# Order of the last out projections in the first mixing, and the point where the second feed-forward's modulation stream starts

## The chip, the core and the metric

One core of a Trainium2 chip runs the whole program. The metric is device time in microseconds (us). The kernel before took 1815.4 us, the median of three runs (1815.14 to 1818.62). Engines are named as in the profile: PE is TensorE's matmul and PEld its weight load, DVE is VectorE, ACT is ScalarE, POOL is GpSimd, SP is the queue that issues nearly all DMAs.

## What is computed

Two layers of a hybrid backbone. A stream of 256 latent tokens `x` and a stream of 256 context tokens `xc`, each 1024 wide, go through: a modulated SwiGLU feed-forward, a token mixing, a second modulated feed-forward. Only the latents are put out, so the context stops after layer 1's keys and values. What matters here is the end of layer 0's mixing and the feed-forward behind it:

```python
x = x + mx[5] * y                      # y = (attention outputs) @ w_out
x = x + 0.5 * mx[8] * swiglu(modulate(rms_norm(x), mx[6], mx[7]), *ffn2)
if need_ctx:                           # layer 0
    xc = xc + mc[5] * y_c
    xc = xc + 0.5 * mc[8] * swiglu(modulate(rms_norm(xc), mc[6], mc[7]), *ffn2)
```

`mx` and `mc` are nine modulation vectors per layer, made from the conditioning vectors by a 1024 by 9216 matrix `w_mod`.

## The kernel before, in words

Activations lie transposed: `xT[k]` holds features 128k to 128k+127 of all 512 tokens, latents in columns 0 to 255 (half `v` = 0), context in 256 to 511 (`v` = 1). Every matmul is done as three, since each operand is split into a high and a low float32r part (`mm3`; the high part is written by ACT, the low part by DVE, or for a few blocks by POOL). A weight block is loaded by `wcols` into `raw` (three buffers), split into `hs` (five buffers), and used by 24 matmuls for each 128 by 512 stretch.

The mixing of layer 0, `mix0`, is a set of named items that `run` carries out in the order of the string `MIX0`. The items `of<dp><v>` are the last out projections: block `dp` of 256 output features, token half `v`. Each has two groups of six matmuls into `ops`, and for each group `residual` adds the result to `xT` (DVE, line 295), squares it (ACT, lines 301 and 304) and adds the square to `ssum` (DVE, line 96). The last item of a half calls `norm_half`: `norm_stats` sums `ssum` over the features with matmuls into `nst`, takes the inverse root (DVE and ACT operations `xe`, `nt`, `rs`), and `norm_bcast` spreads it with two diagonal tiles `dg` (DVE) and two matmuls into `nbc`. `norm_apply` then writes `hT[k]` for k = 0 to 7 with `nrm` (DVE), the high part (ACT) and the low part (DVE). For `v` = 1 that last step is put in a list and run by `flush` inside the first pair of the feed-forward.

`ffn` computes gate (`gps`) and up (`ups`) products pair by pair. Its first pair is "halved": 96 matmuls of 256 columns for the latents, 96 for the context; later pairs have 96 matmuls of 512 columns each.

The modulation vectors that are not needed at the start are computed on DVE: `mod_part` multiplies a row block of `w_mod` with the conditioning vector and sums (`junk`, line 212), one operation for each of the two conditioning vectors. `pump_every` sets how many of these are written behind each block of matmuls. For the second feed-forward of layer 0 the first of them stands behind a gate: a copy of one element of `xT[7][:, 255:256]` into `junk` (line 209), which can only run once that element has its final value.

The code is traced by Python, and a scheduler then lays each engine's instructions into one fixed order by priority and its own idea of when operands are ready; engines carry them out in that order and wait on semaphores. So the table and the gate decide what the scheduler may put where.

At the end of layer 1's mixing, `raw_chunk` writes the un-normed input `hTl` of the last feed-forward chunk by chunk; columns 256 and 257 of `hTl` hold the shift vector twice. They are written by two ACT copies (line 368) and two DVE subtractions (line 369).

Of the kernel before, what the change touches and what calls it, by code (L numbers as in the profile page):

```python
# [8 lines left out]
F32 = mybir.dt.float32  # L9
R32 = mybir.dt.float32r  # L10
I32 = mybir.dt.int32
AF = mybir.ActivationFunctionType
# [6 lines left out]
KC = 8  # L19
SEQ = 256  # L20
NTOK = 512
# [4 lines left out]
HALF = (slice(0, 256), slice(256, 512))  # L26
FFN_PARTS = (6, 5)
MOD_STEP = 1
GATE = lambda xT: xT[7][:, 255:256]


POOL = """of21 od30 of20 oa01 dk00 dv10 uq1 bk11 uk00 oa20 bq00 oa30 aq11 uk01 ob30 ob10 dq00 bk10 oc20 dv11 ob31 oa00
# [20 lines left out]

MIX0 = """g bq00 bk00 f bk01 bv00 bq01 bq10 sb0b sb0a bk10 sb1b sb1a bq11 bv01 rb0 bk11 rb1 sb2a ak0 sb2b bv10 bv11
    sb3a rb2 ak1 aq00 aq01 sb3b rb3 aq10 sa1 sa0 aq11 ob30 sa2 ob31 ob10 ob11 ra0 sa3 ra2 sa4 sa5 ra1 ra3 ob20
    ra4 oa31 sa6 sa7 ob00 ob21 oa10 ob01 oa30 ra6 oa01 oa21 oa00 ra7 oa11 ra5 oa20 of11 of21 of00 of10 of30 of31
    of01 of20"""
MIX1 = """dq00 cq00 g f dk00 dk01 sd0 sd2 dv00 dv01 cq20 rd0 sd1 sd3 cq10 dk10 cqn dq10 rd2 dk11 sd6 rd1 uq0 dv10 dv11
    sd5 sd4 sd7 ckv0 rd4 rd3 ckv1 uk10 rd5 uk00 rd6 uk11 rd7 uk01 uq1 sc0 rc0 od00 sc1 sc2 sc4 sc3 od10 sc6 rc1
    rc2 sc5 od20 rc3 sc7 rc4 rc6 rc5 oc00 rc7 oc30 oc20 of20 of30 of00 oc10 of10 od30"""  # L60
# [3 lines left out]
def tile_hybrid_dit(ctx: ExitStack, tc: tile.TileContext, I, out, dbg=None):  # L64
    nc = tc.nc
    V, S, T, Q = nc.vector, nc.scalar, nc.tensor, nc.sync
# [72 lines left out]
    def const(name, shape, src=None):  # L139
        n = math.prod(shape[1:])  # L140
        at, size = place.get(SHARED.get(name), (sum(z for _, z in place.values()), n))
        assert n <= size and at + n <= NCONST
        if name not in SHARED:
            place[name] = at, n
        t = call[:, at:at + n]
        if len(shape) > 2:
            ax = "abcd"[:len(shape) - 1]
            t = t.rearrange(f"p ({' '.join(ax)}) -> p {' '.join(ax)}", **dict(zip(ax, shape[1:])))
        if src is not None:
            Q.dma_start(out=t, in_=src)  # L150
        return t
# [13 lines left out]
    modT = const("modT", [P, 2, 2, 9, KC])  # L165
# [25 lines left out]
    def needs_ctx(l, m):  # L191

        return l == 0 or m < 5
# [11 lines left out]
    def mod_part(l, m, k, raw):  # L205

        junk = rawp.tile([P, D], F32, tag="junk", name="junk", bufs=1)
        if mod_gate[0] is not None:
            V.tensor_copy(junk[:, 0:1], mod_gate[0])
            mod_gate[0] = None  # L210
        for v in range(2 if needs_ctx(l, m) else 1):
            V.tensor_tensor_reduce(out=junk, in0=raw, in1=mod_c[v], scale=0.5 if m in (2, 8) else 1.0,  # L212
                                   scalar=bT[:, l, m, k:k + 1], op0=ALU.mult, op1=ALU.add,
                                   accum_out=modT[:, l, v, m, k:k + 1])

    def mod_stream():

        raw = None
        while mod_list:
            l, m = mod_list.pop(0)  # L220
            for k in range(KC):
                if raw is None:
                    raw = mod_load(l, m, k)
                    yield
                now, raw = raw, None
                nxt = (l, m, k + 1) if k + 1 < KC else mod_list[0] + (0,) if mod_list else None
                if nxt is not None:
                    raw = mod_load(*nxt)
                mod_part(l, m, k, now)
                if k + 1 == KC:  # L230
                    mod_done.add((l, m))
                yield

    mod_list, mod_gen, mod_gate = [], [None], [None]

    def need(l, *ms):
        while any((l, m) not in mod_done for m in ms):
            pump(1)

    def queue_mods(l, *ms):  # L240
        if not mod_list:
            mod_c.clear()
        mod_list.extend((l, m) for m in ms)
# [39 lines left out]
    xT = [xall[:, k, :] for k in range(KC)]  # L283
    ssum = const("ssum", [P, NTOK])
    hT = [None] * KC
# [74 lines left out]
    hraw = []  # L360

    def raw_chunk(l, m, k):
        need(l, m, m + 1)
        if not hraw:
            hraw.append(hp.tile([P, KC, 2, 264], R32, tag="hTl", name="hTl", bufs=1))
            sh = modT[:, l, 0, m, :].rearrange("p (k o) -> p k o", o=1)
            for c in (256, 257):
                S.activation(hraw[0][:, :, 0, c:c + 1], sh, AF.Copy)
                V.tensor_tensor(out=hraw[0][:, :, 1, c:c + 1], in0=sh, in1=hraw[0][:, :, 0, c:c + 1].bitcast(F32),
                                op=ALU.subtract)  # L370
        h, x, sc = hraw[0][:, k, :, 0:256], xT[k][:, 0:256], modT[:, l, 0, m + 1, k:k + 1]
        S.activation(h[:, 0], x, AF.Copy, scale=sc)
        V.scalar_tensor_tensor(out=h[:, 1], in0=x, scalar=sc, in1=h[:, 0].bitcast(F32), op0=ALU.mult,  # L373
                               op1=ALU.subtract)

# [612 lines left out]
    def mix1():  # L988
# [261 lines left out]
        for h in range(8):  # L1250
            d_unit(h)
            c_unit(h)
        put("", out_items(1, w_out, {"od": (od, 4, (0, 1, 2, 3), None), "oc": (oc, 0, (0, 1), OUT_TAGS[2]),
                                     "of": (oc, 0, (2, 3), OUT_TAGS[3])}, (0,), lambda v: raw_stats(1, 6), lambda k: raw_chunk(1, 6, k)))
        run(items, MIX1)

# [3 lines left out]
    def probe():  # L1260
        if dbg is not None:
            for k in range(KC):
                Q.dma_start(out=dbg[f"x{k}"], in_=xT[k])
# [13 lines left out]
    next(mixing[0], None)  # L1277
    if stop == 1:
        return probe()
    mod_gate[0] = GATE(xT)  # L1280
    queue_mods(0, 8)
    queue_mods(1, 1, 0, 2)
    ffn(0, *w(0, 2), 8, (0, 1), lambda v: norm_half(1, 0, v))
# [58 lines left out]
```

## Time and profile before

| | |
|---|---|
| median of three runs | 1815.4 us |
| the profiled execution's own time | 1815.71 us |
| its span, first to last instruction | 1813.6 us |
| mean granted TensorE clock | 0.993 of 2.4 GHz |
| PE busy, share of the span | 97% |
| DVE busy, share of the span | 67% |
| ACT busy, share of the span | 41% |

The span is what the trace covers; the 2.1 us between it and the execution's own time lie around it. Times inside the trace are us from the span's start. In a row of the timeline the bracket at the end names how long the engine sat idle before that row and which instruction of which engine ended the wait.

### The profile page before, as it was taken

The page shows a single profiled execution, that of the slowest core. Times are in us where ns is not written, and L with a number is a line of the kernel's source. Part 1 is how long each engine was busy: PE and PEld are TensorE (multiplying, and loading weights), DVE is VectorE, ACT ScalarE, POOL GpSimd, SP SyncE. Part 2 cuts the span into 40 slices and gives each one's busy share as a digit, 9 for nine tenths or more (in the row PEclk, how much of TensorE's full clock was granted, in tenths as well). Part 3 has the DMA queues.
Part 4 walks back from the last instruction along what each step waited for, and adds up shares of the span by engine and source line. Part 5 has one row for each costly group of instructions (what it writes and reads, how often), then busy time and mean ns, then how long its engine had stood idle before and what let it go on. Part 6 is the DMA issues. An engine that isn't in the chain of part 4 may idle for free.

```text
span 1813.6 us, 26777 instructions
## 1 busy us (share of the span) xinstructions
PE 1762.3 (97%) x10563; PEld 1537.5 (85%) x10563; DVE 1220.6 (67%) x2343; ACT 738.8 (41%) x1322; POOL 46.0 (3%) x25
## 2 busy tenths in 40 slices
PE   7999999999999989999999999999999998999999
PEld 5788888898998888888888988888889986789998
DVE  5999953467688699989854633333346787876664
ACT  4333132345666543222233332222334656664442
POOL 0000000011010000000000000000001011000000
PEclk9999999999999989999999999999999999999999
DMA  9777752322110237778863233233233442155552
GB/s 305 273 245 225 236 190 88 116 73 68 50 60 14 59 121 240 241 229 261 300 199 105 81 94 94 92 105 103 88 111 101 89 102 57 47 178 183 175 186 82
DMA packets 214025, 256.90 MB, mean 142 GB/s; under 512 B 21484, under 2 KB 195724, under 8 KB 213900
## 3 DMA queue, kind: packets, MB, share of 16 engines
q1 hardware_dynamic: 213900, 255.19, 45.6%
q8 instruction: 83, 1.36, 0.3%
q14 instruction: 42, 0.34, 0.1%
HBM read 254.11 MB, written 1.05 MB: 141 GB/s over the span
## 4 chain that ended last, share of the span: by engine, by line
PE 87%; DVE 7%; ACT 3%; DMA 2%; issue 1%; SPq 0%; DVEq 0%; ACTq 0%
PE ups L103 23%; PE gps L103 23%; PE dps L103 23%; PE ops L103 3%; PE po L756 2%; PE sc L103 2%; DVE hs L100 1%; DMA bias<-in_d_rpb_dram 1%; PE trp L659 1%; PE pbk L103 1%; PE pbv L103 1%; PE paq L103 1%; PE pbq L103 1%; PE ptl L724 1%; PE mps L524 1%
## 5 line engine op out<-in xcount | busy, mean ns | idle before, releaser
L100 DVE TENSOR_TENSOR hs<-raw,hs 128x1024 fp32r<-128x1024 f32 (+2 forms) x308 | 367.9, 1200 | 284.1 <-ACT hs L99 283.4
L99 ACT ACTIVATE hs<-raw 128x1024 fp32r<-128x1024 f32 (+2 forms) x308 | 314.9, 1030 | 541.4 <-PE dps L103 177.8
L103 PE MATMUL dps<-ah,hs 128*128 128x512 f32 (+1 forms) x2256 | 401.0, 338 | 0.2 <-DVE hs L100 0.2
L103 PEld LDWEIGHTS dps<-ah,hs 128*128 128x128 f32 x2256 | 350.6, 190 | 46.4 <-DVE hs L100 0.4
L103 PE MATMUL gps<-hT,hs 128*128 128x512 f32 (+1 forms) x1680 | 375.3, 380 | 4.9 <-ACT hT L542 2.7
L103 PE MATMUL ups<-hT,hs 128*128 128x512 f32 (+1 forms) x1680 | 371.6, 377 | 0.0
L103 PEld LDWEIGHTS gps<-hT,hs 128*128 128x128 f32 x1680 | 305.0, 190 | 65.5 <-ACT hT L542 3.5
L103 PEld LDWEIGHTS ups<-hT,hs 128*128 128x128 f32 x1680 | 303.3, 188 | 58.8 <-issue 1.0
L212 DVE CUSTOM_DVE_ANT_0 junk<-mraw,cb,const 128x1024 f32<-128x1024 f32 x224 | 283.6, 1283 | 16.3 <-DMA mraw<-in_k_w_modT_dram 11.1
L99 ACT ACTIVATE ah<-af 128x512 fp32r<-128x512 f32 (+1 forms) x88 | 50.4, 574 | 127.5 <-DVE af L93 93.9
L295 DVE SCALAR_TENSOR_TENSOR xT<-dps,const,xT 128x256 f32<-128x256 f32 x112 | 50.3, 480 | 77.0 <-PE dps L103 76.9
L276 POOL TENSOR_TENSOR hs<-raw,hs 128x1024 fp32r<-128x1024 f32 (+2 forms) x21 | 45.8, 2186 | 1558.2 <-ACT hs L275 1493.8
L93 DVE TENSOR_TENSOR af<-sg,ups 128x512 f32<-128x512 f32 x66 | 45.2, 685 | 41.0 <-PE ups L103 40.9
L103 PE MATMUL gps<-hTl,hs 128*128 128x258 f32 x528 | 66.8, 284 | 1.6 <-DVE hTl L373 1.0
L428 ACT ACTIVATE sg<-gps 128x512 f32<-128x512 f32 x66 | 38.9, 589 | 70.2 <-PE gps L103 70.2
L103 PEld LDWEIGHTS gps<-hTl,hs 128*128 128x128 f32 x528 | 64.7, 190 | 2.5 <-DVE hTl L373 1.2
L103 PE MATMUL ups<-hTl,hs 128*128 128x258 f32 x528 | 65.5, 283 | 0.0
L103 PEld LDWEIGHTS ups<-hTl,hs 128*128 128x128 f32 x528 | 64.4, 190 | 0.0
L100 DVE TENSOR_TENSOR ah<-af,ah 128x512 fp32r<-128x512 f32 (+1 forms) x88 | 54.6, 621 | 13.2 <-ACT ah L99 13.2
L684 DVE TENSOR_REDUCE nm<-sc 128x1 f32<-128x512 f32 (+1 forms) x80 | 53.8, 682 | 5.0 <-PE sc L103 4.6
L690 ACT ACTIVATE pr<-sc,nm 128x512 f32<-128x512 f32 (+1 forms) x64 | 40.3, 634 | 13.7 <-DVE nm L684 13.4
L304 ACT ACTIVATE sq<-xT 128x256 f32<-128x256 f32 (+1 forms) x54 | 23.6, 449 | 50.9 <-DVE xT L295 50.6
(296 smaller groups left out, 1894.3 us busy)
## 6 DMA issues: line engine op xcount, KB each, us to landing
mraw<-in_k_w_modT_dram SPq DMA_DIRECT2D x128, 512.0 KB, 4.6
raw<-in_ffn_w_gate_dram SPq DMA_DIRECT2D x88, 512.0 KB, 4.7
raw<-in_ffn_w_up_dram SPq DMA_DIRECT2D x88, 512.0 KB, 4.5
raw<-in_ffn_w_down_dram SPq DMA_DIRECT2D x80, 512.0 KB, 4.1
raw<-in_cd_w_in_dram SPq DMA_DIRECT2D x18, 512.0 KB, 3.8
wm<-in_w_mod_dram SPq DMA_DIRECT2D x16, 512.0 KB, 8.7
raw<-in_ab_w_in_dram SPq DMA_DIRECT2D x16, 512.0 KB, 3.8
raw<-in_ffn_w_down_dram SPq DMA_DIRECT2D x16, 256.0 KB, 2.7
```

Source lines behind the costliest of these rows:

```text
L93: V.tensor_tensor(out=out_, in0=a, in1=b, op=ALU.mult)
L99: S.activation(h, src, AF.Copy)
L100: V.tensor_tensor(out=l, in0=src, in1=h.bitcast(F32), op=ALU.subtract)
L103: T.matmul(ps, a, b, start=start, stop=stop)
L212: V.tensor_tensor_reduce(out=junk, in0=raw, in1=mod_c[v], scale=0.5 if m in (2, 8) else 1.0, scalar=bT[:, l, m, k:k + 1], op0=ALU.mult, op ...
L276: nc.gpsimd.tensor_tensor(out=hs[:, 1, :n], in0=raw[:, :n], in1=hs[:, 0, :n].bitcast(F32), op=ALU.subtract)
L295: V.scalar_tensor_tensor(out=xT[dc][:, a:e], in0=ps[:, a:e], scalar=modT[:, l, v, m, dc:dc + 1], in1=xT[dc][:, a:e], op0=ALU.mult, op1=ALU ...
L304: S.activation(sq[:, cols], xT[dc][:, cols], AF.Square)
L428: S.activation(sg, g[:, :ntok], AF.Silu)
L684: V.tensor_reduce(out=nm[:, c], in_=view, axis=AX.X, op=ALU.max, negate=True)
L690: S.activation(p[:, cols], sc[:, cols], AF.Exp, bias=nm[:, i + b:i + b + 1], accum_out=den[:, i + b:i + b + 1])
L756: T.matmul(po[64 * x:64 * x + 64, q], val(x, c), pts[x][c], start=c == order[0], stop=c == order[-1], tile_position=(0, 64 * x))
```

## The change

Three things. First, `MIX0` ends with the four latent items of the last out projections and then the four context items, where the two halves were mixed before. Second, the gate in front of the modulation stream of layer 0's second feed-forward copies an element of the last chunk of `hT` (low part, last context token) instead of an element of `xT`; it is a function now, since `hT` is only allocated inside the mixing. Third, in `raw_chunk` the columns 256 and 257 of `hTl` are written after the first chunk's ACT operation, held there by `tc.issue_after`, and the two subtractions follow them.

```diff
-GATE = lambda xT: xT[7][:, 255:256]
...
 MIX0 = """g bq00 bk00 f bk01 bv00 bq01 bq10 sb0b sb0a bk10 sb1b sb1a bq11 bv01 rb0 bk11 rb1 sb2a ak0 sb2b bv10 bv11
...
-    ra4 oa31 sa6 sa7 ob00 ob21 oa10 ob01 oa30 ra6 oa01 oa21 oa00 ra7 oa11 ra5 oa20 of11 of21 of00 of10 of30 of31
-    of01 of20"""
+    ra4 oa31 sa6 sa7 ob00 ob21 oa10 ob01 oa30 ra6 oa01 oa21 oa00 ra7 oa11 ra5 oa20 of00 of10 of30 of20 of11 of21
+    of31 of01"""
...
         if mod_gate[0] is not None:
-            V.tensor_copy(junk[:, 0:1], mod_gate[0])
+            V.tensor_copy(junk[:, 0:1], mod_gate[0]())
             mod_gate[0] = None
...
             hraw.append(hp.tile([P, KC, 2, 264], R32, tag="hTl", name="hTl", bufs=1))
+        h, x, sc = hraw[0][:, k, :, 0:256], xT[k][:, 0:256], modT[:, l, 0, m + 1, k:k + 1]
+        first = S.activation(h[:, 0], x, AF.Copy, scale=sc).ins
+        if len(hraw) == 1:
+            hraw.append(first)
             sh = modT[:, l, 0, m, :].rearrange("p (k o) -> p k o", o=1)
             for c in (256, 257):
-                S.activation(hraw[0][:, :, 0, c:c + 1], sh, AF.Copy)
+                with tc.issue_after(first):
+                    S.activation(hraw[0][:, :, 0, c:c + 1], sh, AF.Copy)
...
-        h, x, sc = hraw[0][:, k, :, 0:256], xT[k][:, 0:256], modT[:, l, 0, m + 1, k:k + 1]
-        S.activation(h[:, 0], x, AF.Copy, scale=sc)
...
-    mod_gate[0] = GATE(xT)
+    mod_gate[0] = lambda: hT[KC - 1][:, 1, NTOK - 1:NTOK].bitcast(F32)
```

What this does to the fixed orders, at three places. On PE, the last matmuls of the mixing; `ops` are the out projections, `nst` the sums of squares (6258 and 6172 the latents', 6329 the context's). Before:

```order
L103 MATMUL ops1_6207<-oa_6030,hs_6112 128x256 x3
L103 MATMUL ops1_6207<-oa_5977,hs_6112 128x256 x3
L103 MATMUL ops0_6228<-oa_6030,hs_6085 128x256 x3
L103 MATMUL ops0_6228<-oa_5977,hs_6085 128x256 x3
L103 MATMUL ops1_6229<-oa_6030,hs_6085 128x256 x3
L103 MATMUL ops1_6229<-oa_5977,hs_6085 128x256 x3
L103 MATMUL nst_6258<-const_79 128x1 x2
L103 MATMUL nst_6329<-const_79 128x1 x2
L103 MATMUL nbc_6270<-dg_6271,const_79 128x128
```

All out projections stand ahead of both halves' sums. On the same engine at the same place, now:

```order
L102 MATMUL ops0_6265<-oa_6030,hs_6112 128x256 x2
L102 MATMUL nst_6172<-const_79 128x1 x2
L102 MATMUL ops0_6265<-oa_6030,hs_6112 128x256
L102 MATMUL ops0_6265<-oa_5977,hs_6112 128x256 x3
L102 MATMUL ops1_6266<-oa_6030,hs_6112 128x256 x3
L102 MATMUL ops1_6266<-oa_5977,hs_6112 128x256 x3
L102 MATMUL ops0_6287<-oa_6030,hs_6060 128x256 x3
L102 MATMUL ops0_6287<-oa_5977,hs_6060 128x256 x3
L102 MATMUL ops1_6288<-oa_6030,hs_6060 128x256 x3
L102 MATMUL ops1_6288<-oa_5977,hs_6060 128x256 x3
L102 MATMUL nbc_6184<-dg_6185,const_79 128x128
```

The latents' sums now stand 22 matmuls ahead of the end of the out projections, and the context's sums have gone from here. On PE, inside the latents' gate products of the first pair (`hs_6311` and `hs_6321` are the gate's two weight blocks, for chunks 0 to 3 and 4 to 7). Before:

```order
L103 MATMUL gps1_6381<-hT_6253,hs_6311 128x256 x2
L103 MATMUL gps0_6380<-hT_6254,hs_6321 128x256 x3
L103 MATMUL gps1_6381<-hT_6254,hs_6321 128x256 x3
L103 MATMUL gps0_6380<-hT_6255,hs_6321 128x256 x3
L103 MATMUL gps1_6381<-hT_6255,hs_6321 128x256 x3
```

The gate products run through. The same place now:

```order
L102 MATMUL gps0_6380<-hT_6168,hs_6321 128x256 x2
L102 MATMUL gps1_6381<-hT_6168,hs_6321 128x256 x2
L102 MATMUL nst_6329<-const_79 128x1 x2
L102 MATMUL gps0_6380<-hT_6168,hs_6321 128x256
L102 MATMUL gps1_6381<-hT_6168,hs_6321 128x256
L102 MATMUL gps0_6380<-hT_6169,hs_6321 128x256 x3
L102 MATMUL gps1_6381<-hT_6169,hs_6321 128x256 x3
L102 MATMUL gps0_6380<-hT_6170,hs_6321 128x256 x3
L102 MATMUL gps1_6381<-hT_6170,hs_6321 128x256 x2
L102 MATMUL nbc_6341<-dg_6342,const_79 128x128
```

The context's sums stand in the middle of the latents' gate products, 28 matmuls in, and its spread 13 matmuls later. On DVE, between the latents' sums and the first `nrm` (`hs_6316`, `hs_6321` and `hs_6326` are the low parts of three of the first pair's four weight blocks; `sq_6247` is the last square of a half). Before:

```order
L100 TENSOR_TENSOR hs_6316<-raw_6314,hs_6316 128x1024
L96 TENSOR_TENSOR const_79<-const_79,sq_6247 128x256
L100 TENSOR_TENSOR hs_6321<-raw_6319,hs_6321 128x1024
L128 TENSOR_SCALAR xe_6262<-nst_6258 128x2
L100 TENSOR_TENSOR hs_6326<-raw_6324,hs_6326 128x1024
L131 SCALAR_TENSOR_TENSOR nt_6263<-rs_6261 128x2
L128 TENSOR_SCALAR xe_6333<-nst_6329 128x2
L93 TENSOR_TENSOR nt_6263<-nt_6263,xe_6262 128x2
L209 COPY junk_6442<-xT_99 128x1
L133 SCALAR_TENSOR_TENSOR rs_6261<-nt_6263,rs_6261 128x2
L212 ISA junk_6442,const_79<-mraw_6390,cb_6384,const_79 128x1024
L212 ISA const_79 128x1
```

Three block splits, the gate and the first modulation operation stand ahead of the latents' `dg`, and a second one ahead of their `nrm`. Now these splits stand behind the latents' whole `hT`, just ahead of the context's `nrm`:

```order
L294 SCALAR_TENSOR_TENSOR xT_99<-ops1_6288,const_79,xT_99 128x256
L99 TENSOR_TENSOR hs_6316<-raw_6314,hs_6316 128x1024
L95 TENSOR_TENSOR const_79<-const_79,sq_6306 128x256
L99 TENSOR_TENSOR hs_6321<-raw_6319,hs_6321 128x1024
L99 TENSOR_TENSOR hs_6326<-raw_6324,hs_6326 128x1024
L127 TENSOR_SCALAR xe_6333<-nst_6329 128x2
L130 SCALAR_TENSOR_TENSOR nt_6334<-rs_6332 128x2
L92 TENSOR_TENSOR nt_6334<-nt_6334,xe_6333 128x2
L132 SCALAR_TENSOR_TENSOR rs_6332<-nt_6334,rs_6332 128x2
L322 TENSOR_SCALAR dg_6342<-const_79,rs_6332 128x128
L322 TENSOR_SCALAR dg_6345<-const_79,rs_6332 128x128
L99 TENSOR_TENSOR hs_6618<-raw_6616,hs_6618 128x1024
```

The context's last addition (`sq_6306`) stands behind the latents' 16 norm operations and one split; `hs_6618`, a block of the second pair, has come in front of the context's `nrm`; the gate and all modulation operations follow the context's last `hT`. From the second pair on the orders hold the same work; at the same weight block DVE has two to four modulation operations less behind it than before, until the stream ends at the same block.

## Rows read from the trace of the kernel before

**Rows 1.** The profile's page: the span, the shares of the chain of work that ended last, and of the DMA issues the row of the gate blocks (count, KB of each, median us from issue to landing).

```profile
span 1813.6 us, 26777 instructions
...
PE 87%; DVE 7%; ACT 3%; DMA 2%; issue 1%; SPq 0%; DVEq 0%; ACTq 0%
...
raw<-in_ffn_w_gate_dram SPq DMA_DIRECT2D x88, 512.0 KB, 4.7
```

**Rows 2.** Busy time of PE, PEld, DVE, ACT and POOL in two stretches, then the granted clock, the DMA share and GB/s: the end of the mixing, and the steady feed-forward behind it.

```profile
645.00:655.00 10.00, 2.75 (x14) 2.40 (x14) 10.00 (x25) 3.77 (x11) 0.00 (x0) 0.73 0.55 168
...
680.00:720.00 40.00, 40.00 (x181) 33.19 (x180) 38.91 (x57) 14.39 (x19) 0.00 (x0) 1.00 0.77 242
```

**Rows 3.** The timeline of PE from the last out projections to the second pair (start us, us, instruction, count, and in brackets the wait before it).

```profile
631.63 13.21 PE L103 MATMUL ops<-oa,hs 128*128 128x256 f32 x108
647.89 1.05 PE L103 MATMUL nst<-const 128*128 128x1 f32 x8 [3.06 <-DVE const L96]
652.19 1.20 PE L103 MATMUL nbc<-dg,const 128*128 128x128 f32 x4 [3.24 <-DVE dg L323]
654.50 8.44 PE L103 MATMUL gps<-hT,hs 128*128 128x256 f32 x48 [1.12 <-ACT hT L354]
...
680.50 9.71 PE L103 MATMUL gps<-hT,hs 128*128 128x512 f32 x42
```

**Rows 4.** The timeline of DVE in the same stretch.

```profile
645.21 0.49 DVE L295 SCALAR_TENSOR_TENSOR xT<-ops,const,xT 128x256 f32<-128x256 f32 x1
645.61 0.76 DVE L96 TENSOR_TENSOR const<-const,sq 128x256 f32<-128x256 f32 x2
646.27 1.23 DVE L100 TENSOR_TENSOR hs<-raw,hs 128x1024 fp32r<-128x1024 f32 x1
647.41 0.43 DVE L96 TENSOR_TENSOR const<-const,sq 128x256 f32<-128x256 f32 x1
...
650.56 1.28 DVE L212 CUSTOM_DVE_ANT_0 junk<-mraw,cb,const 128x1024 f32<-128x1024 f32 x1
...
651.76 0.48 DVE L323 TENSOR_SCALAR dg<-const,rs 128x128 f32<-128x128 f32 x2
...
652.22 1.28 DVE L212 CUSTOM_DVE_ANT_0 junk<-mraw,cb,const 128x1024 f32<-128x1024 f32 x1
...
653.43 1.26 DVE L352 SCALAR_TENSOR_TENSOR nrm<-xT,const,nbc 128x256 f32<-128x256 f32 x3
654.61 1.27 DVE L355 SCALAR_TENSOR_TENSOR hT<-nrm,const,hT 128x256 fp32r<-128x256 f32 x3
...
660.21 0.88 DVE L355 SCALAR_TENSOR_TENSOR hT<-nrm,const,hT 128x256 fp32r<-128x256 f32 x2
```

**Rows 5.** The timelines of ACT (first two rows) and of SP's queue (last row) there; the SP row is the issue of two gate blocks of the second pair.

```profile
651.40 1.06 ACT L99 ACTIVATE hs<-raw 128x1024 fp32r<-128x1024 f32 x1 [0.61 <-DMA raw<-in_ffn_w_gate_dram]
653.94 1.30 ACT L354 ACTIVATE hT<-nrm,const 128x256 fp32r<-128x256 f32 x3 [1.48 <-DVE nrm L352]
...
647.57 1.85 SPq L269 DMA_DIRECT2D raw<-in_ffn_w_gate_dram  x2
```

**Rows 6.** The chain of work that ended last, in order of time, in the stretch where the first feed-forward of layer 0 ends (start us, us, what): the latents' norm of the mixing, with the context's down projections behind it.

```profile
385.32 0.58 PE nst L103 x4
385.90 2.02 PE dps L103 x16
387.92 0.46 PE nbc L103 x4
388.38 0.02 issue
388.40 1.26 DVE nrm L352 x3
```

**Rows 7.** Short stretches in which the granted clock (the third number from the end) fell or rose; columns as in rows 2.

```profile
427.50:428.00 0.50, 0.09 (x1) 0.12 (x2) 0.50 (x2) 0.50 (x2) 0.00 (x0) 0.68 1.07 381
430.50:431.00 0.50, 0.50 (x4) 0.50 (x4) 0.00 (x0) 0.50 (x1) 0.00 (x0) 0.50 0.00 0
431.00:431.50 0.50, 0.50 (x6) 0.50 (x6) 0.00 (x0) 0.49 (x2) 0.00 (x0) 0.91 0.14 33
...
649.50:650.00 0.50, 0.00 (x0) 0.00 (x0) 0.50 (x1) 0.02 (x1) 0.00 (x0) 0.54 1.03 367
...
659.50:660.00 0.50, 0.50 (x5) 0.50 (x4) 0.50 (x1) 0.13 (x1) 0.00 (x0) 0.72 0.00 0
```

**Rows 8.** The timeline of PE behind two waits inside the first mixing.

```profile
427.91 0.66 PE L659 MATMUL trp<-const,hsq 128*128 128x128 f32 x2 [2.12 <-DVE hsq L100]
...
538.91 0.44 PE L659 MATMUL trp<-const,hsq 128*128 128x128 f32 x2 [2.45 <-DVE hsq L100]
```

**Rows 9.** The chain that ended last, two pieces of it: six matmuls of 256 columns in the first pair, and the down projections of the first part (288 matmuls of 512 columns, 12 weight blocks).

```profile
666.26 0.72 PE gps L103 x6
...
789.49 65.65 PE dps L103 x288
```

**Rows 10.** What runs on line 369 (count, ns shortest/median/longest, first and last start), and PE's longest wait at the end of the second mixing.

```profile
L369 DVE TENSOR_TENSOR hTl<-const,hTl x2: 169/169/169, 908.8 to 908.9; 128x8 fp32r<-128x8 f32 x2
...
1614.55 3.51 PE L103 MATMUL gps<-hTl,hs 128*128 128x258 f32 x24 [1.02 <-DVE hTl L373]
```

**Rows 11.** The reload of the conditioning vector for the next batch of modulations: the timeline of ACT and of DVE.

```profile
789.71 1.06 ACT L200 ACTIVATE cb<-cb 128x1024 f32<-128x1024 f32 x1 [4.57 <-DMA cb<-in_c_dram]
...
790.80 1.28 DVE L212 CUSTOM_DVE_ANT_0 junk<-mraw,cb,const 128x1024 f32<-128x1024 f32 x1 [3.31 <-ACT cb L200]
```

**Rows 12.** The longest sum in the list of SP's own waits between 600 and 1060 us (engine, line, awaited: us in total, times, longest us).

```profile
SPq L269 <- DVE hs L100: 188.2, 68, 12.5
```

## The prediction

> **What bounds the kernel now.** I read the page first: the chain that ended last lies 87% on PE, so the time moves by what PE waits, and by little else [rows 1]. Next the busy times by stretch: the feed-forward behind the mixing keeps PE at 40.00 of 40.00 us with the clock at 1.00, while the ten microseconds at the end of the mixing hold 2.75 us of PE and DVE is busy throughout [rows 2]. So the change can only win in that hole or lose in places that now have no hole. The timelines of PE and DVE give the hole its steps. The out projections end at 644.84. PE waits 3.06 us for the last addition to `ssum`, 3.24 us for `dg`, 1.12 us for the first `hT`; then 48 matmuls take 8.44 us, which at 0.12 each would be 5.8, since `hT` comes slowly and the clock is low [rows 3, 9]. The first 512-column product starts at 680.50, and from there PE runs without waits. Hence I walk PE and DVE from the last out projections to that start; its shift is the main term. DVE goes by the distance of starts, not by the durations shown, which overlap: residual 0.40, addition 0.33, split 1.14, modulation operation 1.21, `nrm` or low part 0.395, `dg` pair 0.46 [rows 4].
>
> **The latents' norm.** Nine items of 12 matmuls take 13.21 us, 0.122 per matmul [rows 3]. The last latent item is now the fifth of nine here, so six of the context's residual-and-addition pairs (0.73 each) come off DVE ahead of the latents' last addition: 645.21 − 4.4 + 0.4 = 641.2. The sums stand 86 matmuls in, 631.63 + 86 × 0.122 = 642.1, so their wait of 3.06 goes. DVE mixes the four small operations with context work, and PE's out projections end at 644.84 + 0.5 for the four sums now among them, 645.3; I put `dg` at 645.1 and `nbc` at 645.5. From `nbc` to `nrm` the earlier norm took 0.48 [rows 6]; with an operation in flight on DVE, first `nrm` 646.2 instead of 653.43: 7.2 earlier. It can't be before 645.8, since PE gets to `nbc` no sooner than 645.3. First product 1.07 behind it, as before [rows 3, 4]: 647.3. What made up the 7.2: the earlier sums, three splits (3.4) and two modulation operations (2.4), less context work that now lies between.
>
> **The context's norm, where it comes back.** The 16 norm operations at 0.395 fill DVE to 652.5; before they took 653.43 to 661.09 with a modulation operation among them [rows 4]. Then two additions (0.66), the last residual (0.40), `hs_6316` (1.14) and the last addition (0.33): 655.1. PE meets the context's `nst` 28 matmuls into the gate products; these are paced by `hT` and end about 651.2. **So PE waits 3.9 us, in a place where before it waited for nothing.** Sums at 655.15 to 655.7. The 13 products behind them need `hs_6321`'s low part, 656.3, and end at 657.9. DVE does `hs_6326` to 657.4, then the chain to `dg`, 658.3; `nbc` 658.7; the next products from 659.2. Of the pair's 192 short matmuls 41 are done, 151 × 0.12 = 18.1 are left [rows 9]: 677.3 against 680.50. **−3.2 us.**
>
> **The clock.** Before, it fell at 649.5 to 650.0 (0.54) with PE idle and was back to 0.72 in 659.5 to 660.0; twice inside the mixing it fell in a pause of 2.12 and 2.45 us and was low until 431.0 in the first of them, some 3.4 us [rows 7, 8]. My pause is longer, so I expect one fall. The 13 products and the spread at half speed cost 1.25; if the clock holds until 655.7, nothing. I take **+0.6**, halfway, since the fall begins inside the wait and most of the low time lies in it.
> The Trainium skill ("TensorE: Matmul & The Clock Gate", section "HAM oscillation — how this bites in real kernels") speaks against the change here: pauses inserted between short runs of matmuls each cost the clock again, and products should be run through before PE waits. Rows 7 and 8 agree that short pauses cost it (0.50 behind waits of 2.12 and 2.45 us); without the fall the sum would be 0.6 lower, with a second one it is the second rival below.
>
> **The moved block and its DMA.** `hs_6618` needs `raw_6616`, which is issued on SP only when `hs_6316` is split: 654.9 instead of 647.57. It landed at 651.40, 3.83 later; ACT takes 1.06, DVE 1.14 [rows 4, 5]: 661.0. The context's `nrm` stands behind it, first `hT` 1.07 later at about 662.1 to 662.7. PE does the 31 gate products that are left for the latents, and reaches the context at 659.2 + 31 × 0.12 = 662.9. Cost zero, with 0.2 to 0.8 us to spare. The page's median landing, 4.7, would use that up [rows 1]. What queues behind this issue on SP (weight rows for the modulation, next blocks) comes some 7 us later; the second pair starts at 677.3, so its first block, split by 661, has 16 us in hand. POOL has nothing here [rows 2].
>
> **Modulation stream and the reload.** All modulation operations start behind both norms, two to four fewer per block, 2.4 to 4.8 us of DVE work that must be made up before the stream's end; there is room for that: 38.91 of 40 busy counts an operation at 1.28 where starts lie 1.21 apart, so DVE is really idle for about 40 − 38.91 × 1.21 / 1.28 = 3.2 us in 40 [rows 2, 4], and the order ends the stream at the same block. The place where a late stream could bite is the reload of `cb`: ACT waited 4.57 us for it and DVE 3.31 [rows 11]. ACT's splits stand behind it in order, but four blocks are then split ahead, each worth 65.65 / 12 = 5.5 us of PE [rows 9], some 22 us. Cost zero; if that cover were gone, 4.6.
>
> **`hTl` columns.** Two subtractions of 0.169 us leave a place where they cost nothing and go to the end of the second mixing, where PE waited 1.02 us for DVE's `hTl` [rows 10]. If both stand ahead of that wait: 2 × 0.169 = 0.34; if neither, 0. **+0.2**, between, since their starts lie closer than their lengths.
>
> **Sum.** −3.2 + 0.6 + 0.2 = −2.4; the profiled execution of 1815.71 becomes 1813.3. It stands 0.3 above the median of 1815.4, so the forecast for a median is **1813.0**. A measurement of this kernel tells about 0.2%, 3.6 us, from no change: faster means below 1811.8, slower above 1819.0.
>
> **Rivals.**
> *The context's norm costs less.* If DVE runs its norm work at 0.33 (no modulation beside it), 16 × 0.065 = 1.0 goes, the first `nrm` at 645.8 gives 0.4, and the clock and columns 0.8 more: 1810.8. With no wait left at all the products behind `nbc` would start 5.2 earlier, at 672.1: 1807.2. For: each DVE step was read where splits and modulation ran. Against: the order puts the last addition behind 16 norm operations and a split, whatever they take.
> *The gain is given back.* The clock stays low to 662 as it stayed ten microseconds before: 0.65 more for the short products and half of 2.8 us behind 659.2, together +2.05: 1815.0. A landing of 4.7 or more adds some tenths. For: PE gets pauses at 642 to 647 and at 651, and the fall of 649.5 lasted that long [rows 7]. Against: between these two pauses matmuls run.
> *Slower: the second pair's block holds up the context.* `hs_6618` now blocks DVE until its DMA has come, and every microsecond past a landing of about 4.6 is one of PE. SP waits in order for DVE's splits, longest 12.5 us [rows 12]; if issue and landing here took 12.5 together, 7.9 past that point, and −2.4 stands against it: +5.5, 1820.9. For: the queue is in order, and the DMA engines are 0.55 busy there at 168 GB/s [rows 2]. Against: 3.83 was measured in just that stretch, with the modulation's rows on the same queue.
> *The change doesn't do what it says.* The waits only swap and the end of the pair stays at 680.50: 1815.4.
>
> **How the numbers follow.** Forecast, 1811.2 to 1814.2: 0.57, of which 0.07 lies below 1811.8. Context's norm cheaper, 1807.2 to 1811.2: 0.18. Given back, 1814.2 to 1816.0: 0.15. Slower mechanism, 1816 to 1821: 0.07, of which 0.05 above 1819. No effect: 0.03. Faster 0.18 + 0.07 = 0.25; slower 0.05; same 0.70. The range runs to 1810.0 (leaving out about half of the cheaper case, 0.09) and 1816.0 (leaving out 0.07).
>
> **What the profile after would show.** Right: out projections end near 645; the latents' `nst` at 642 without a wait; first `gps` at 647.3; a wait of about 4 us ahead of the second `nst` near 655, released by DVE's addition; a clock below 1 there; the first 512-column product near 678. PE still at 40.00 of 40.00 in the steady stretch; `hTl` at the end later by up to 0.34. Wrong, if the second `nst` waits under 2 us (first rival), if the context's `nrm` starts behind 662 with `hs_6618` just ahead (third), or if waits appear at the reload of `cb`.

## The result, and the profile after

The changed kernel took 1828.0 us, median of four runs (1823.4 to 1828.8), against 1815.4: slower, ratio 1.006 (95% interval 1.004 to 1.008). The forecast was 1813.0 in a range of 1810.0 to 1816.0. The profiled execution is the shortest of the four: 1823.43 us, span 1821.4, 7.8 us above the span of before. No trace covers the other three, which took 4.2 to 5.3 us longer at a mean granted clock of 0.989 to 0.993 against 0.994; what follows accounts for the 7.8.

First the stretch that the prediction walked through. PE's timeline after the change, answering [rows 3]:

```profile
631.54 10.58 PE L102 MATMUL ops<-oa,hs 128*128 128x256 f32 x86
641.96 0.50 PE L102 MATMUL nst<-const 128*128 128x1 f32 x4
642.32 2.87 PE L102 MATMUL ops<-oa,hs 128*128 128x256 f32 x22
645.29 0.71 PE L102 MATMUL nbc<-dg,const 128*128 128x128 f32 x4
647.15 4.22 PE L102 MATMUL gps<-hT,hs 128*128 128x256 f32 x28 [1.14 <-ACT hT L353]
655.05 0.61 PE L102 MATMUL nst<-const 128*128 128x1 f32 x4 [3.69 <-DVE const L95]
656.19 3.14 PE L102 MATMUL gps<-hT,hs 128*128 128x256 f32 x13 [0.53 <-DVE hs L99]
659.13 1.05 PE L102 MATMUL nbc<-dg,const 128*128 128x128 f32 x4
659.84 3.53 PE L102 MATMUL ups<-hT,hs 128*128 128x256 f32 x18
...
679.10 11.18 PE L102 MATMUL gps<-hT,hs 128*128 128x512 f32 x48
```

Nearly every step stands where it was put, and the first 512-column product comes 1.3 us earlier, counted from the first of these out projections (47.56 us instead of 48.87). The loss is elsewhere. Four more starts on PE, of before and then of after, cut the rest of the span: the first long run of gate products, the first products of the first mixing (`pbq`), the last down projections ahead of the second mixing, and the first product with `hTl` behind it.

```profile
59.35 10.27 PE L103 MATMUL gps<-hT,hs 128*128 128x512 f32 x44 [1.13 <-DVE hs L100]
399.08 2.44 PE L103 MATMUL pbq<-hs,hT 128*128 128x256 f32 x19
1329.24 11.04 PE L103 MATMUL dps<-ah,hs 128*128 128x512 f32 x48
1611.94 0.88 PE L103 MATMUL gps<-hTl,hs 128*128 128x258 f32 x6
```

```profile
58.64 10.36 PE L102 MATMUL gps<-hT,hs 128*128 128x512 f32 x44 [1.16 <-DVE hs L99]
400.48 2.41 PE L102 MATMUL pbq<-hs,hT 128*128 128x256 f32 x19
1333.77 11.04 PE L102 MATMUL dps<-ah,hs 128*128 128x512 f32 x48
1619.53 0.88 PE L102 MATMUL gps<-hTl,hs 128*128 128x258 f32 x6
```

By subtraction, after less before: up to the out projections −0.1; from there to the first 512-column product −1.3; feed-forwards up to 1329 **+5.9**; second mixing **+3.1**; from `hTl` to the end +0.2. The sum is the 7.8. The −0.1 hides a loss: the first feed-forward, from 59.35 to 399.08 before, takes **+2.1**. Against it, the changed kernel gets there 0.7 earlier, and its first mixing up to the out projections takes 1.5 less, with 3.4 us at half clock in place of 6.8.

In these feed-forwards PE has no waits worth naming in either kernel. What differs is the count. Two stretches of the busy times after the change (columns as in [rows 2]), and one of before that was not shown:

```profile
680.00:720.00 40.00, 40.00 (x176) 32.70 (x175) 38.68 (x57) 13.82 (x18) 0.00 (x0) 1.00 0.77 245
1080.00:1140.00 60.00, 60.00 (x262) 48.71 (x261) 20.41 (x23) 15.65 (x21) 0.00 (x0) 1.00 0.30 91
```

```profile
1080.00:1140.00 60.00, 60.00 (x267) 49.67 (x266) 21.49 (x23) 17.93 (x23) 0.00 (x0) 1.00 0.32 97
```

PE is busy all the time at the full clock, but does 262 matmuls in 60 us instead of 267. (The 176 against 181 of [rows 2] overstate it: before, four short matmuls of the first pair still start in that stretch, after the change none.) The costliest groups of the page say which (busy us, mean ns); after, then before:

```profile
L102 PE MATMUL dps<-ah,hs 128*128 128x512 f32 (+1 forms) x2256 | 400.1, 338 | 0.2 <-DVE hs L99 0.2
L102 PE MATMUL gps<-hT,hs 128*128 128x512 f32 (+1 forms) x1680 | 379.8, 382 | 5.6 <-ACT hT L544 2.6
L102 PE MATMUL ups<-hT,hs 128*128 128x512 f32 (+1 forms) x1680 | 377.7, 381 | 0.0
```

```profile
L103 PE MATMUL dps<-ah,hs 128*128 128x512 f32 (+1 forms) x2256 | 401.0, 338 | 0.2 <-DVE hs L100 0.2
L103 PE MATMUL gps<-hT,hs 128*128 128x512 f32 (+1 forms) x1680 | 375.3, 380 | 4.9 <-ACT hT L542 2.7
L103 PE MATMUL ups<-hT,hs 128*128 128x512 f32 (+1 forms) x1680 | 371.6, 377 | 0.0
```

Gate and up products, which read `hT`, take 10.6 us more; down projections, which don't, 0.9 less. It begins in the first feed-forward, 500 us ahead of anything that the change moves on PE (the built programs' matmul orders are the same up to the last out projections), so it can't be order or waiting. What the change could alter there is where tiles lie in SBUF: the kernel leaves addresses to a packer, which works from all tiles' lives. The built programs list every tile's place; of the 2818 names that stand in both, 1654 have another. These are `hT`'s (byte in the partition, matmuls of 512 columns that read there):

```
before  121696 120   125792 372   129888 372   162656 372   166752 372
        170848 372   174944 372   179040 372   183136 252
after    16512 120    20608 372    24704 120    28800 372   121696 120   125792 372
        129888 372   162656 372   166752 252   170848 252   174944 252
```

`hTl` lies at 16512 to 33408 in both. Before, its two columns were written near 909 us [rows 10], so its place was reserved from then on. Written late, the place is free for most of the program, and 984 products now read `hT` there. From the starts of neighbouring matmuls in the trace: normal distance 226.7 ns; the 967 that read `hT` at the bottom 6.9 ns more, the rest of `hT` 1.4 more, all of it in the up to seven products that follow a slow one. Summed over the trace, the excess is 9.5 us after and 1.2 before.

The second mixing has a new wait. PE, two rows of DVE, and SP's own longest wait between 1406 and 1426, after the change; the last row is SP's there before, between 1402 and 1418:

```profile
1444.25 0.48 PE L726 MATMUL ptl<-const,pr 128*128 128x128 f32 x1 [3.15 <-DVE pr L712]
...
1434.94 0.69 DVE L95 TENSOR_TENSOR bias<-bias,const 128x512 f32<-128x512 f32 x1 [7.71 <-DMA bias<-in_d_rpb_dram]
...
1423.56 1.23 DVE L99 TENSOR_TENSOR hs<-raw,hs 128x1024 fp32r<-128x1024 f32 x1
...
SPq L268 <- DVE nt L92: 18.2, 1, 18.2
...
SPq L269 <- DVE hs L100: 13.7, 1, 13.7
```

The softmax waits for a bias that lands late, because SP issued it late: the weight block directly ahead of it waited 18.2 us, until a split on DVE ended at 1424.79 (the list puts it down to `nt`, a short operation beside that split); before, it waited 13.7. The order on SP at this point is that of before. What has changed is which block follows which in one place: by the built programs this block now takes the place of the block three ahead of it instead of four ahead, and that one is split 4.2 us later.

### The profile page after: what moved, and what is told of

Read it like the earlier page. It is cut to its first block, busy times and chain, and to the rows that moved or that the text cites. A ratio compares the mean times of both kernels' runs of the same rounds, so it can differ in the third digit from the quotient of the medians.

```text
span 1821.4 us, 26782 instructions
## 1 busy us (share of the span) xinstructions
PE 1771.1 (97%) x10563; PEld 1537.0 (84%) x10563; DVE 1219.5 (67%) x2343; ACT 739.6 (41%) x1322; POOL 45.8 (3%) x25
## 4 chain that ended last, share of the span: by engine, by line
PE 86%; DVE 7%; ACT 3%; DMA 2%; issue 1%; SPq 0%; ACTq 0%; DVEq 0%
PE ups L102 24%; PE gps L102 23%; PE dps L102 23%; PE ops L102 3%; PE po L758 2%; PE sc L102 2%; DVE hs L99 1%; DMA bias<-in_d_rpb_dram 1%; PE pdk L102 1%; PE paq L102 1%; PE trp L661 1%; PE ptl L726 1%; PE pdq L102 1%; ACT hs L98 1%; PE mps L526 1%
## 5 line engine op out<-in xcount | busy, mean ns | idle before, releaser
L102 PE MATMUL gps<-hT,hs 128*128 128x512 f32 (+1 forms) x1680 | 379.8, 382 | 5.6 <-ACT hT L544 2.6
L102 PE MATMUL ups<-hT,hs 128*128 128x512 f32 (+1 forms) x1680 | 377.7, 381 | 0.0
L692 ACT ACTIVATE pr<-sc,nm 128x512 f32<-128x512 f32 (+1 forms) x64 | 40.4, 635 | 18.6 <-DVE nm L686 16.6
```

The costliest lines, as they stand in the source:

```text
L102: T.matmul(ps, a, b, start=start, stop=stop)
L692: S.activation(p[:, cols], sc[:, cols], AF.Exp, bias=nm[:, i + b:i + b + 1], accum_out=den[:, i + b:i + b + 1])
```

## The experiments

Each number of the last four columns is from the profiled execution: A, from the last `po` product of the first mixing to the first 512-column gate product; the excess over 226.7 ns, summed; M, the second mixing, from its first `pdv` to its first product with `hTl`; "low", the time within M that was granted half the clock. "64" says whether the 512-column moving operands and weights of the feed-forwards start alike with respect to 64 bytes.

```
run                              median  ratio [95%]             64       A      excess   M       low
before                           1815.4                          all but 60  49.18  1.2   204.99    6.8
after                            1828.0  1.006  [1.004, 1.008]   984 not  47.87    9.5   208.13   10.2
columns late only                1830.2  1.0071 [1.0059, 1.0084] 984 not  49.05    9.5   212.80   17.1
table and gate                   1817.4  1.0002 [0.9992, 1.0012] 60 not   47.77    1.2   207.39   10.2
all three, place held            1818.5  1.0010 [1.0001, 1.0018] 60 not   47.52    1.2   209.82   17.1
before, 32 bytes on              1817.8  1.0008 [0.9999, 1.0017] all      49.17    0.3   205.47    6.8
after, 32 bytes on               1819.6  1.0008 [1.0000, 1.0017] all      47.51    0.3   208.65    6.8
before, weights 32 bytes on      1839.4  1.0119 [1.0106, 1.0132] 4068 not 48.98   20.5   210.35   13.7
table only                       1818.5  1.0010 [1.0000, 1.0020] 60 not   50.83    1.2   205.75    6.8
gate only                        1815.6  0.9991 [0.9982, 1.0000] 60 not   47.87    1.3   204.46    6.8
gate, 32 bytes on                1815.9  0.9991 [0.9981, 1.0002] all      47.89    0.3   206.51   10.2
  + two context items behind     1815.3  0.9991 [0.9979, 1.0002] all      46.39    0.3   207.81   13.7
  + three context items behind   1815.4  0.9986 [0.9974, 0.9997] all      46.23    0.3   206.19    6.8
gate, 32 on, columns late        1818.8  1.0010 [1.0001, 1.0020] all      47.88    0.3   209.81   13.7
```

From the third row on, ratios are to runs of the kernel before on the same chip at the same time, whose medians were 1816.4 to 1817.1; its single executions spread from 1813.6 to 1821.6, with the clock falling in other pauses each time. So ratios and stretches are compared, not medians of different rows. A repeats well: the four kernels with old table and old gate show 48.98 to 49.18. M does not: up to half of its low time is lost, and that time differs from execution to execution (13.7 us with two context items behind, which has no new wait), so a difference of 2 to 5 us in M alone shows little.

**Which part: the late columns alone.** The third part of the diff, put into the kernel before.

> The kernel before with the third part of the change alone: columns 256 and 257 of hTl written behind the first chunk. Theory A, place in SBUF: hTl's 16.9 KB at the bottom of SBUF stay free until the second mixing ends, other tiles move in, 984 of the 2976 matmuls of 512 columns that read hT read it there, and the gate and up products slow down as in the profile after (10.6 us more of PE busy): 1825 to 1829 us, 512-column gps at 392 ns or a spacing of 233 ns in place of 227. Theory B, order of work: all that moves is 0.34 us of DVE work at the end of the second mixing: 1815.4 to 1815.8 us, and the loss of the changed kernel comes from its first two parts.

1830.2 us, the whole loss, with the excess of the changed kernel to the tenth (9.5). Theory B falls. The mixing lost even more here (M +7.8), with waits of 3.1 us for a weight split and 1.9 for a bias; 10.3 us more at half clock are part of it.

**The other two parts.** The third part undone; then all three, with `hTl`'s place held by an early write:

```diff
             hraw.append(hp.tile([P, KC, 2, 264], R32, tag="hTl", name="hTl", bufs=1))
+            V.tensor_copy(hraw[0][:, 0, 1, 258:259], modT[:, l, 0, m, 0:1])
```

> The changed kernel without its third part: new table and new gate, hTl's columns written early as before. Theory A: hT keeps the places it had before, so the gain that was walked through in the prediction shows alone, -3.2 + 0.6 without the 0.2: 1812.8 us, between 1811.5 and 1814. Theory B: the loss of the changed kernel stays, 1823 to 1828 us.

> The changed kernel with all three parts and one more DVE copy of one column into an unused column of hTl, which can run as early as the columns before could; so hTl's place is held, while its columns 256 and 257 are still written at the end of the second mixing. Theory A: the same as the kernel with table and gate alone, plus 0 to 0.35 us: 1813.0 us. Theory B (or: the late columns themselves cost the time): 1823 to 1828 us.

Both lose the excess, so it is the place and not the late columns that costs. But neither is at 1813: A is 1.4 and 1.7 us shorter, and M 2.4 and 4.8 us longer, of which 3.4 and 10.3 us more at half clock can make up 1.7 and 5.1. In both, one bias of the second mixing takes a place that softmax tiles have just held; before, its last holder, a square of the norm ahead of the mixing, was done by then. SP waits for it (for `rd`), 4.2 us; what this costs PE was not isolated. The row is of the kernel with table and gate:

```profile
SPq L1053 <- DVE rd L697: 4.2, 1, 4.2
```

**What is wrong with the bottom place.** `NCONST = 3636` made 3644 shifts everything behind the constants by 32 bytes; the third kernel shifts the weights alone.

```diff
-            hs = hsp.tile([P, 2, 1024], R32, tag="hs", name="hs")
+            hs = hsp.tile([P, 2, 1040], R32, tag="hs", name="hs")[:, :, 8:1032]
```

> The kernel before with 8 unused columns added to the constants' tile; this shifts every tile that lies behind it in SBUF by 32 bytes, so that all start at a multiple of 64 bytes, as the tiles at the bottom did before (the others started 32 bytes past one). No instruction order changes. Three forms of theory A: if a start at a multiple of 64 bytes is what makes a 512-column matmul slow, all 2976 + 1224 of them take 7 ns more, +29 us, 1844 us; if the bottom of SBUF is, nothing changes, 1815.4 us; if it is that moving operand and weights start differently with respect to 64 bytes, the 60 slow ones of the down projections become fast, 1815.0 us.

> The changed kernel with the constants' tile 8 columns wider, so that all of SBUF behind it starts at a multiple of 64 bytes, as the bottom does; no instruction order changes, hT stays at the bottom for 984 matmuls. Theory A1, weights and moving operand that start differently with respect to 64 bytes make a 512-column matmul slow: all now start alike, the spacing behind hT at the bottom falls from 233.6 to 227 ns, the excess from 9.5 to 0.3 us, and the time from 1828 to 1818 to 1820 us; what is left against before is the waits in the second mixing. Theory A2, the bottom of SBUF itself is slow: 1828 us as it is.

> The kernel before with each weight block's halves laid 32 bytes further into a block that is 128 bytes longer, so that weights start at a multiple of 64 bytes while hT and nearly all ah start 32 bytes past one; the same instructions in the same order. Theory A1: 2976 + 1092 matmuls of 512 columns take 7 ns more, +28 us, about 1845 us. Theory A2, or a rule on the moving operand alone: the time of before, 1815 to 1818 us.

The 32 bytes alone left the time of the kernel before where it was, within the noise (1.0008, interval 0.9999 to 1.0017; the third form had 1815.0, the median was 1817.8). The bottom is not slow in itself. At the bottom tiles start at a multiple of 64 bytes, elsewhere 32 past one, and weights lay elsewhere. Once all start alike, the 60 slow matmuls of before and the 984 of after take the normal time (the 965 recorded: 0.17 ns over it), and the changed kernel comes down to 1819.6, as expected. With weights moved against everything else, same orders, 20.5 us of excess appear; expected were 28, since here it is 4.9 ns per matmul and not 7. So all four pairs of starts were measured: alike at 0 or alike at 32 past a multiple of 64, fast; apart in either direction, slow. The count shows it in the stretch that was compared above:

```profile
1080.00:1140.00 60.00, 60.00 (x261) 48.65 (x260) 20.77 (x23) 17.90 (x22) 0.00 (x0) 1.00 0.26 79
```

**Table and gate apart.**

> The kernel before with the new table alone; the old gate lets modulation operations stand ahead of the norms, and the bias and weight blocks of the second mixing have the SBUF places of before. By the steps of the prediction the first 512-column product of the second feed-forward comes 0 to 1.5 us earlier, counted from the last scores of the first mixing. By theory A (places set the waits in the second mixing) no wait of 2 us or more appears there around 1440 us, and the total is 1814.5 to 1817 us.

> The kernel before with the new gate alone: the two modulation operations ahead of the latents' dg and nrm (2.4 us of DVE) go behind both norms, the sums stay behind all out projections. By the steps of the prediction the first 512-column product comes 1 to 2.4 us earlier. The bias tiles have other SBUF places than before, freed by down projections alone (no DVE operation of the second mixing), so by theory A the second mixing has no new wait: 1813.5 to 1816.5 us.

The gate alone gives A its 1.3 us, and its mixing is not longer. The table alone makes A 1.65 us longer, not shorter: PE waits 3.68 us for the context's sums as in the changed kernel, and then 2.74 for the context's `dg`, since with the old gate three modulation operations (1.21 each) stand between its sums and it. Its total, 1818.5, lies above the 1814.5 to 1817 that were expected, while no `ptl` waits 1 us, as expected. So with the gate in place, the table adds nothing measurable: 47.87 without and 47.5 to 47.9 with it.

**Tables that avoid the context's wait**, with the gate and the 32 bytes.

> The kernel before with the new gate and with the constants' tile 8 columns wider, so that weights and all moving operands start at a multiple of 64 bytes. The gate brings 1.3 us (measured in the run with the gate alone), the 60 slow matmuls and the drain behind them 0.9 us of excess less; nothing is lost in the second mixing, where no weight or bias block takes a place that is still in use. Theory: 2.2 us below before, ratio 0.9988, which a measurement can hardly tell from none.

> As the run before it, and a third table: the latents' four items end two context items ahead of the end (of11 of21 of00 of10 of30 of20 of31 of01). Here the context's last addition stands ahead of the latents' nrm on DVE and its sums directly behind the latents' spread on PE. If it is the context's last addition, queued behind the latents' 16 norm operations and a split, that cost PE 2.4 to 3.7 us in the changed kernel, that wait is gone, but the latents' dg waits for one split and four additions again: first 512-column product 2 to 3 us earlier than before, counted from the last scores of the first mixing; total ratio 0.998. If the context's norm is not the cause, about the 1.3 us of the gate alone.

> As the run with gate and 8 columns more, and a fourth table: three context items behind the latents' last (of11 of00 of10 of30 of20 of21 of31 of01). The context's last addition stands behind 14 of the latents' 16 norm operations and no split, so its sums come about 3 us earlier than in the changed kernel, while the latents' norm hides behind 36 matmuls of the context. First 512-column product 2.5 to 3.5 us earlier than before, PE waiting less than 1.5 us for the context's sums; total ratio 0.9975 to 0.998.

Both tables bring A down by 2.8 and 2.95 us, as expected; their totals are not (0.9991 and 0.9986 against 0.998 and 0.9975 to 0.998). PE's timeline with three context items behind the latents:

```profile
630.26 12.13 PE L102 MATMUL ops<-oa,hs 128*128 128x256 f32 x99
642.67 0.61 PE L102 MATMUL nst<-const 128*128 128x1 f32 x4 [0.28 <-DVE const L95]
643.13 1.37 PE L102 MATMUL ops<-oa,hs 128*128 128x256 f32 x9
646.25 1.04 PE L102 MATMUL nbc<-dg,const 128*128 128x128 f32 x4 [1.74 <-DVE dg L322]
648.40 5.88 PE L102 MATMUL gps<-hT,hs 128*128 128x256 f32 x28 [1.11 <-ACT hT L353]
654.11 0.50 PE L102 MATMUL nst<-const 128*128 128x1 f32 x4
655.23 2.65 PE L102 MATMUL gps<-hT,hs 128*128 128x256 f32 x20 [0.62 <-DVE hs L99]
658.36 0.71 PE L102 MATMUL nbc<-dg,const 128*128 128x128 f32 x4 [0.47 <-DVE dg L322]
```

The second `nst` waits for nothing, where the changed kernel waited 3.69. This is the one version whose interval lies wholly below 1, by 0.14%, less than the 0.2% that such a measurement was said to tell; what is clear is the 2.95 us within the stretch, and that it beats the changed kernel (0.9986 against 1.006).

**What is left of the late columns when starts are alike.** The gate kernel with 32 bytes, and the third part of the change.

> As the run with the new gate and the constants' tile 8 columns wider, but with hTl's columns written late as in the changed kernel; table as before. Everything starts at a multiple of 64 bytes, so hT at the bottom costs nothing per matmul. What is left of the third part: the weight blocks of the second mixing lie in their places in another rotation, and one of them now waits on SP for the split that GpSimd does late, with the bias loads queued behind it. Theory: PE waits 2.5 to 4 us near 1437 us for ptl behind a bias that lands late, and the total is 2 to 4 us above the run without late columns, 1818 to 1820 us. Rival, only the starts counted: the same as the run without late columns, 1815 to 1816.5 us, plus 0.35 at most.

The ratio rises from 0.9991 to 1.0010, M by 3.3 us (3.5 us more at half clock among them), and PE's wait before its first `ptl` is the one expected:

```profile
1441.62 0.33 PE L726 MATMUL ptl<-const,pr 128*128 128x128 f32 x1 [3.84 <-DVE pr L712]
...
DVE bias L95 <- DMA bias<-in_d_rpb_dram: 9.2, 2, 7.7
```

The expectation had the reason wrong in part: the weight block ahead of the biases waits 18.6 us for a split on DVE, as in the changed kernel, and not on GpSimd. At equal low time, the changed kernel with the 32 bytes has an M 3.2 us above that of the kernel before with them (208.65 against 205.47). So the third part has two costs, both by places: slow products, and a transfer queue that waits for an earlier user of a buffer.

## Why the prediction was wrong

- **The latents' norm: right.** Sums 641.96 (642.1), spread 645.29 (645.5), first `nrm` 646.08 (646.2), first product 647.15 (647.3).
- **The context's norm: right.** The wait was 3.69 us at 655.05 for DVE's addition (3.9 at 655.1); the 13 products began at 656.19 (656.3). No wait followed at the context's half, so `hs_6618` and its DMA cost nothing, as put, and the rival built on it did not happen. (Of the 31 "gate products" that cover it, 24 are `up` products; the count is right.)
- **The clock: one fall, as put, but placed wrongly and mis-sized.** The prediction took half of 1.25, since "the fall begins inside the wait and most of the low time lies in it", and put a clock that holds until 655.7 at no cost. The clock was full throughout the wait (1.00 in 645 to 655), fell at 655.6, half a microsecond behind the wait's end, and was at half until 662.4: nearly all of its low time lay on work. The first `up` products start 0.6 late (659.84 against 659.2) and lose half of the 2.6 us to 662.4 again, 1.9 in all instead of 0.6. That is why A gained 1.3 us and not 2.6. This was the mechanism of the rival that the gain is given back; its price was inside the range.
  The Trainium skill (TensorE: Matmul & The Clock Gate, "HAM oscillation — how this bites in real kernels") warns of pauses between short runs of matmuls, and the trace agrees with it here: 0.55 at 655.5.

```profile
645.00:655.00 10.00, 4.97 (x34) 4.02 (x32) 10.00 (x27) 4.78 (x12) 0.00 (x0) 1.00 0.00 1
655.50:656.00 0.50, 0.16 (x2) 0.07 (x1) 0.50 (x1) 0.00 (x0) 0.00 (x0) 0.55 0.27 47
662.00:662.50 0.50, 0.50 (x5) 0.50 (x5) 0.50 (x2) 0.50 (x2) 0.00 (x0) 0.62 0.79 131
```

- **Modulation stream and reload: right.** PE has no wait of note from there to the second mixing.
- **The `hTl` columns: the step that failed.** The prediction priced two subtractions, "+0.2", and they cost that (0.2 from `hTl` to the end). "Two subtractions of 0.169 us leave a place where they cost nothing" was wrong: the early write was what reserved 16.9 KB of SBUF. Setting that free moved `hT` (excess +8.3 us) and the places of the second mixing's loads (+3.1 us there, of which 3.4 us more at half clock can make up 1.7). A gain of 1.3 where 2.6 was put, and 2.2 us that the start and the first mixing took less, stand against it.
- **A check that could not have shown it.** The prediction wanted PE "still at 40.00 of 40.00" in the steady stretch. It was. A busy share says that PE never waits, not how fast it goes; the count in a stretch of equal work, 267 and 262, does.

Shown by experiments: that the third part makes the loss, that it does so through places, that different starts with respect to 64 bytes make 512-column products slow in either direction, and that the gate makes the gain. Argued from trace and built program, not isolated further: that the bias waits come from the reuse of one place. In the four kernels with late columns and `hTl`'s place free, the block ahead of the biases follows the later split, and a `ptl` waits 1.9 to 3.8 us; in the other ten it doesn't, and no `ptl` waits 1 us. But other places differ in these four too. Not walked through: the 4.6 us between the profiled execution and the median. Open: what in the chip makes operands with different starts slow, and why by 6.9 ns one way and 4.9 the other.

## What to carry to other kernels

Where a packer chooses addresses, moving a tile's first write or last read can change where most tiles lie (1654 of 2818 names here), and with it the rate of matmuls that aren't touched and the buffers that queues wait for. Read the built program's places beside the order, and compare matmul counts per stretch, not busy shares, in code that was not changed. When a small gain is sought, hold the places still (an early write held `hTl`'s here, though a bias still moved) and measure the stretch by itself: here 1 to 3 us were clear within the stretch, while whole runs spread by 8.

## What was not expected of the hardware

In these runs a 512-column float32r matmul starts 226.7 ns behind the one before it when weights and moving operand start alike with respect to 64 bytes, and 231.6 to 234 ns when one of them lies 32 bytes off. Products of 258 columns show no such cost: 704 of the 1056 with `hTl` start 32 bytes apart from their weights in the kernel before and stand 120.4 ns apart; with the 32 bytes the same 704 start alike and stand 120.9 apart.
